# A sixth seven-product pair in each feed-forward duo of a decoder trunk, with a new order of its weight sums

## The chip, the cores and the metric

The kernel runs on one core of one Trainium2 chip. Its time is the device time in microseconds of one execution; runs of the kernel before gave 2178.22, 2179.26 and 2179.58 us, a median of 2179.26 us. The core has a matrix engine (PE, with its weight loads as PEld), a vector engine (DVE), an activation engine (ACT), GpSimd (POOL), a queue that issues transfers (SP), and DMA engines that move data from HBM.

## The reference, cut to what matters

```python
D_MODEL = 2048; SEQ = 256; D_FF = 5632      # one sequence of 256 tokens, float32

def swiglu(h, w_gate_up, w_down):
    gate, up = jnp.split(h @ w_gate_up, 2, axis=-1)
    return (jax.nn.silu(gate) * up) @ w_down

# layer 0: x += norm(GLA(norm(x)));        x += norm(swiglu(norm(x)))
# k, v = split(rmsnorm(x) @ w_kv)
# layer 1: x += norm(DiffAttn(norm(x)));   x += norm(swiglu(norm(x)))
```

Two layers, each a token mixer and a feed-forward block (SwiGLU). Each block has the products gate and up (2048 by 5632 each) and down (5632 by 2048). The change is in both feed-forward blocks and, in one detail, at the norm in front of the shared keys and values.

## The kernel before, in words

**Products.** Every float32 operand is split into a high and a low part (`hi`, `lo`, both float32r), and a product of a 128x128 piece of the activations with a 128x512 piece of the weights is three matmuls: high by high, high by low, low by high. Those three are called a product here. The activations are the stationary operand, the weights stream; a matmul streams 512 columns into an accumulator (`acc`, or `tp` where a transpose bank is borrowed).

**The weight stream.** Weights arrive in order as raw tiles of 128x1024 (two k-tiles of 512 columns, 512 KB each), issued from SP into five buffers (`NRAW`). Each becomes a unit: ACT copies the raw tile into `hi` (line 294), DVE subtracts it from the raw tile into `lo` (line 296), and PE uses both. Up to nine units are made ahead of PE (`NRING`). `take` hands a unit to PE and makes more, `free` gives its places back.

**A duo.** A chunk is 512 columns of gate or up. Eleven chunks each of gate and up make a block; chunk 0 is done by itself, and chunks 1 to 10 as duos: gate chunk c with up chunk 11+c, for both token halves (128 rows each), in eight steps s of two k-tiles. A plain step takes two units, one raw tile of each matrix, and does eight products. A fast step, or pair, computes the same with seven products on sums of weights and of activations (Strassen's scheme on a 2x2 block): its four units are a (the first raw tile as it is), b, c (1024 wide) and d (512 wide, in narrow places), where b, c and d are made of sums of the two raw tiles: DVE adds four 128x512 pieces (line 317, `sums`). The sums of activations are built once a block (`build_forms`, line 546). `FAST_FFN` lists the pairs of a duo, five of eight; chunk 1 has four (`FAST_SECOND`).

**After the steps.** When the last pair is done, DVE and ACT take five of the duo's seven accumulators apart (`early`, line 1129), and after step 7 the others (`late`), then Silu on ACT and gate times up on DVE (line 1133). PE transposes the result later (line 609), ACT and DVE split it (lines 611, 612).

**The order of a block.** Between two duos stands one part of the down products: eight units, twelve matmuls each (lines 370 to 372), with the running sums copied into accumulators by ACT before (line 423) and out after (line 1203). So from chunk 2 on the block is a row of nine spans, one duo with one part of down.

**What orders the instructions.** The program is written in the order PE consumes; helpers are put off by a count of ticks (`defer`), and a list scheduler with a cost model then sets the order on each engine. Each engine works its queue in order. `high_priority` lifts a helper, `issue_after(ins)` puts instructions of the same engine behind `ins` in the order, without a wait.

**The norm before the shared keys and values.** At the end of the first block the last units of down are skewed: all of the first token half, then all of the second. For each half, `after` calls the norm: DVE adds the block's output to x, PE transposes it, ACT and DVE scale and split it into `h_kv` (`scaled_T`, lines 644 to 650). PE then begins the value product with `h_kv`.

Of the kernel before, what the change touches and what calls it, by code (L numbers as in the profile page):

```python
# [18 lines left out]
P = 128  # L19
# [21 lines left out]
FAST_FFN = (0, 2, 3, 4, 6)  # L41
# [6 lines left out]
NRAW, NRING = 5, 9  # L48
V_BEGIN, V_EVERY, V_Q = 16, 3, 1
# [137 lines left out]
class Trunk:  # L187
    def __init__(self, ctx, tc, t):
# [16 lines left out]
        self.subs = {}  # L205
        self.raws = {}
# [83 lines left out]
    def split(self, src, gp=False):  # L290
        nc = self.nc
        w = src.shape[-1]
        hi, lo = self.places(w)
        nc.scalar.copy(hi, src)  # L294
        eng = nc.gpsimd if gp else nc.vector
        eng.tensor_tensor(out=lo, in0=src, in1=hi.bitcast(F32), op=ALU.subtract)  # L296
        return hi, lo
# [26 lines left out]

    def convert(self):
        n = self.n_conv
        kind = self.stream[n][2]
        self.n_done += kind in ("plain", "beside", "c", "b")
        if kind == "plain":
            self.subs[n] = self.split(self.raw(), n in self.pool_lo) if n else self.split_halves(self.raw())  # L330
        elif kind == "beside":
            self.subs[n] = self.split_beside(self.raw())
        elif kind == "a":
# [15 lines left out]
    def take(self, name, idx, kind="plain"):  # L349
# [4 lines left out]
        return self.subs.pop(n)  # L354

# [93 lines left out]
    def duo_act(self, aT, forms, fast, c1, c2, early, late):  # L449

        ps = [self.acc() for _ in range(6)] + [self.tp().rearrange("p j t -> p (j t)")]
        for s in range(8):
            k1, k2 = 2 * s, 2 * s + 1
            if s in fast:
# [18 lines left out]
                if last:  # L473
                    early(ps)
                continue
            for (w, n), pair in ((c1, ((1, 0), (3, 1))), (c2, ((4, 1), (2, 2)))):
                wp = self.take(w, (n, s))
                for bank, which in pair:
# [3 lines left out]
                    if s == 7:  # L482
                        late(bank, ps)
# [4 lines left out]
    def duo_apart(self, aT, forms, fast, chunks, early, late):  # L488
# [9 lines left out]
        for s in range(8):  # L498
            k1, k2 = 2 * s, 2 * s + 1
            if s not in fast:  # L500
                for (w, n), banks in zip(chunks, ((1, 3), (2, 7))):
                    wp = self.take(w, (n, s))
                    for b, bank in enumerate(banks):
# [4 lines left out]
                        if s == 7:  # L508
                            late(bank, ps)
                        self.tick()  # L510
                continue
            f, last = forms.pairs.index(s), s == fast[-1]
            plan = {
                "a": ((0, aT.tokens(k1, 0)), (1, aT.tokens(k2, 0))),
                "b": ((6, forms.fast(f, 2)), (2, forms.fast(f, 3))),
                "c": ((4, forms.fast(f, 0)), (3, aT.tokens(k2, 1))),
                "d": ((5, forms.fast(f, 1)),),
# [8 lines left out]
            if last:  # L526
                early(ps)
# [111 lines left out]

    def scaled_T(self, dst, b, c, xc, gi, plain=None):  # L640
# [8 lines left out]
        for j in range(4):  # L649
            nc.vector.scalar_tensor_tensor(  # L650
                out=lo[:, j, :], in0=tp[:, j, :], scalar=g[j], in1=hi[:, j, :].bitcast(F32),
                op0=ALU.mult, op1=ALU.subtract,
            )
        if plain is not None:
# [505 lines left out]
    def ffn(self, fp, hT, rs, gi, wgu, wd, post, after, name, reload, side=None):  # L1160
        nc = self.nc
        self.narrow, self.n_narrow = (fp, 0, 3), 0
# [10 lines left out]
        def gate_T(sg, c):  # L1173
# [3 lines left out]
            for b in range(2):  # L1177
                self.split_T(gTs[grp], 4 * grp.index(c), sg[:, b, :], b)
# [36 lines left out]
        for n, (kind, which, *chunks) in enumerate(plan):  # L1215
# [21 lines left out]
            def done(c, b, ps, grp=which):  # L1237
                (self.urgent(evac) if skew else evac)(grp, c, b, ps)
# [348 lines left out]
```

## Time and profile before

| | before |
|---|---|
| median of three runs | 2179.26 us |
| profiled execution | 2178.21 us |
| its span, first to last instruction | 2176.5 us |
| PE busy | 2161.2 us (99%) |
| DVE busy | 1889.5 us (87%) |
| ACT busy | 1341.4 us (62%) |
| transferred | 440.09 MB, 202 GB/s |

The profile is of one execution. Busy is the time in which an engine had at least one instruction under way; the durations of neighbours overlap, so the spacing of two starts is shorter than a duration. "Idle before" of an instruction is the engine's idle time just ahead of it, and the name behind the arrow is what ended it. Shares over the whole span mix stages of different limits, so a stage is read from its own window.

### The profile page before, as it was taken

To read this page: it belongs to the slowest core of one execution; us is meant where nothing else is said; L and a number is where in the kernel's file an instruction comes from. 1 tells how busy PE (TensorE), PEld (TensorE's weight loads), DVE (VectorE), ACT (ScalarE), POOL (GpSimd) and SP (SyncE) were. 2 spreads that over 40 slices of the span, in tenths; PEclk is the share of its full clock that TensorE was granted. 3 is DMA by queue.
4 is the path that set the end of the run, shared out by engine and by line. 5 is a ranking of instruction groups with operands and counts; after the bars stand their busy time and mean duration, and the time that the engine had idled before them with its cause. 6 is when DMAs were issued, how large, how long until landed. Compare 5 with 4: busy or idle time off the path is not lost.

```text
span 2176.5 us, 28464 instructions
## 1 busy us (share of the span) xinstructions
PE 2161.2 (99%) x10098; PEld 1797.6 (83%) x10098; DVE 1889.5 (87%) x2566; ACT 1341.4 (62%) x1888; POOL 36.3 (2%) x66
## 2 busy tenths in 40 slices
PE   9999999999999999999999999999999999999998
PEld 7887788888888888888788888888888888888886
DVE  7989988999899989988798567889998999899985
ACT  8656655666656666666676455556566666666664
POOL 1000000000000000000000000000000000000000
PEclk9999999999999999999999999999999999999999
DMA  8546566667655566565757655465656556566664
GB/s 309 168 150 191 176 228 212 215 212 246 204 179 193 198 213 212 195 222 191 239 189 245 189 172 164 149 233 195 230 197 221 189 178 197 204 209 220 204 212 136
DMA packets 123315, 440.09 MB, mean 202 GB/s; under 512 B 13899, under 2 KB 16628, under 8 KB 121380
## 3 DMA queue, kind: packets, MB, share of 16 engines
q1 hardware_dynamic: 121996, 436.44, 60.2%
q10 hardware_dynamic: 1176, 1.84, 0.2%
q8 instruction: 79, 1.29, 0.2%
q14 instruction: 64, 0.52, 0.1%
HBM read 429.82 MB, written 9.97 MB: 202 GB/s over the span
## 4 chain that ended last, share of the span: by engine, by line
PE 98%; DVE 1%; issue 0%; DMA 0%; ACT 0%; POOL 0%; SPq 0%; DVEq 0%; POOLq 0%; ACTq 0%
PE acc L445 13%; PE acc L447 13%; PE acc L446 13%; PE acc L372 11%; PE acc L370 11%; PE acc L371 11%; PE acc L588 8%; PE acc L589 4%; PE tp L445 3%; PE tp L446 3%; PE tp L447 3%; PE tp L609 1%; DVE lo L296 1%; PE acc L1310 0%; PE acc L1349 0%; PE tp L644 0%
## 5 line engine op out<-in xcount | busy, mean ns | idle before, releaser
L294 ACT CAST hi<-raw 128x1024 fp32r<-128x1024 f32 x905 | 929.7, 1051 | 568.2 <-DVE raw L317 227.2
L296 DVE TENSOR_TENSOR lo<-raw,hi 128x1024 fp32r<-128x1024 f32 x903 | 1079.6, 1219 | 182.2 <-ACT hi L294 179.4
L371 PE MATMUL acc<-lo,f_ffn_gT 128*128 128x512 f32 x704 | 273.7, 389 | 0.0
L370 PE MATMUL acc<-hi,f_ffn_gT 128*128 128x512 f32 x704 | 273.1, 390 | 0.0
L372 PE MATMUL acc<-hi,f_ffn_gT 128*128 128x512 f32 x704 | 268.5, 389 | 0.0
L445 PE MATMUL acc<-hi,h_ffn 128*128 128x512 f32 x666 | 259.3, 389 | 0.0
L447 PE MATMUL acc<-hi,h_ffn 128*128 128x512 f32 x666 | 259.3, 389 | 0.0
L446 PE MATMUL acc<-lo,h_ffn 128*128 128x512 f32 x666 | 259.1, 389 | 0.0
L372 PEld LDWEIGHTS acc<-hi,f_ffn_gT 128*128 128x128 f32 x704 | 132.2, 188 | 27.4
L370 PEld LDWEIGHTS acc<-hi,f_ffn_gT 128*128 128x128 f32 x704 | 132.0, 188 | 27.5 <-issue 0.6
L371 PEld LDWEIGHTS acc<-lo,f_ffn_gT 128*128 128x128 f32 x704 | 132.2, 188 | 27.1
L447 PEld LDWEIGHTS acc<-hi,h_ffn 128*128 128x128 f32 x666 | 125.0, 188 | 26.0
L446 PEld LDWEIGHTS acc<-lo,h_ffn 128*128 128x128 f32 x666 | 125.1, 188 | 25.9
L445 PEld LDWEIGHTS acc<-hi,h_ffn 128*128 128x128 f32 x666 | 125.0, 188 | 25.8
L588 PE MATMUL acc<-h_q,hi 128*128 128x512 f32 x256 | 92.6, 402 | 0.0
L588 PE MATMUL acc<-h_kv,hi 128*128 128x512 f32 x256 | 90.6, 399 | 0.0
L588 PE MATMUL acc<-h_mix,hi 128*128 128x512 f32 x256 | 90.6, 398 | 0.0
L317 DVE TENSOR_TENSOR raw<-sum,raw 128x512 f32<-128x512 f32 x122 | 84.3, 691 | 3.8
L317 DVE TENSOR_TENSOR raw<-raw 128x512 f32<-128x512 f32 x122 | 84.3, 691 | 3.6
L317 DVE TENSOR_TENSOR raw<-raw,raw 128x512 f32<-128x512 f32 x122 | 83.9, 687 | 2.3
L1203 ACT COPY f_ffn<-acc 128x512 f32<-128x512 f32 x80 | 46.9, 586 | 60.8 <-PE acc L372 60.6
L317 DVE TENSOR_TENSOR sum<-raw,raw 128x512 f32<-128x512 f32 x122 | 83.4, 684 | 0.0
(412 smaller groups left out, 3966.1 us busy)
## 6 DMA issues: line engine op xcount, KB each, us to landing
raw<-in_w_gu_dram SPq DMA_DIRECT2D x352, 512.0 KB, 4.5
raw<-in_w_d_dram SPq DMA_DIRECT2D x176, 512.0 KB, 4.9
raw<-in_gla_w_r_dram SPq DMA_DIRECT2D x32, 512.0 KB, 4.7
raw<-in_gla_w_v_dram SPq DMA_DIRECT2D x32, 512.0 KB, 4.0
raw<-in_gla_w_out_dram SPq DMA_DIRECT2D x32, 512.0 KB, 4.5
raw<-in_w_v_dram SPq DMA_DIRECT2D x32, 512.0 KB, 4.5
raw<-in_w_k_dram SPq DMA_DIRECT2D x32, 512.0 KB, 4.5
raw<-in_diff_w_q_dram SPq DMA_DIRECT2D x32, 512.0 KB, 4.2
```

The source lines that it names most:

```text
L294: nc.scalar.copy(hi, src)
L296: eng.tensor_tensor(out=lo, in0=src, in1=hi.bitcast(F32), op=ALU.subtract)
L317: nc.vector.tensor_tensor(out=out, in0=in0, in1=in1, op=ALU.add)
L370: nc.tensor.matmul(ps, ah, rh, start=(kt == 0 and not onto), stop=False, skip_group_check=onto)
L371: nc.tensor.matmul(ps, ah, rl, start=False, stop=False, skip_group_check=onto)
L372: nc.tensor.matmul(ps, al, rh, start=False, stop=(kt == 2 * ns - 1), skip_group_check=onto)
L445: nc.tensor.matmul(ps, ah, wh, start=first, stop=False)
L446: nc.tensor.matmul(ps, ah, wl, start=False, stop=False)
L447: nc.tensor.matmul(ps, al, wh, start=False, stop=last)
L588: nc.tensor.matmul(ps, lh, aT.both(kt), start=(kt == 0), stop=False)
L589: nc.tensor.matmul(ps[:, SEQ:], ll, aT.hi(kt), start=False, stop=(kt == KT - 1))
L1203: nc.scalar.copy(fc, ps)
```

## The change

Six things change.

1. `FAST_FFN` gets pair 5: steps 0, 2, 3, 4, 5 and 6 are fast, so that plain steps are 1 and 7 only. The sums of activations of one more pair are built.
2. For the feed-forward duos (weights whose name begins with `w_g`) the four weight sums are made by `convert_ffn`. The first sum goes into the narrow tile `sum` rather than over the raw tile, and is put behind unit a's low part on DVE; the second and fourth stay in place, the third is over the raw tile. Units c and d swap what they carry: the wide one now has bank 5 and form 1 beside bank 3, the narrow one bank 4 and form 0.
3. The narrow units have four places rather than three: two in a pool and two in the rest of a tile (before: three in the rest).
4. `early` and `late` of every duo, those outside the feed-forward blocks too, are put behind the cast and the low part of the latest unit made among those up to three ahead of PE (`behind`).
5. The low parts of weights are put behind the last low part of `h_kv` traced for the first token half (`split_off`, set in `scaled_T` only where x is kept too, which is this norm).
6. `GATE_BEHIND` and `DOWN_BEHIND` are 0 and do nothing.

The diff, cut:

```diff
-FAST_FFN = (0, 2, 3, 4, 6)
+FAST_FFN = (0, 2, 3, 4, 5, 6)
+EARLY_BEHIND, LATE_BEHIND, DOWN_BEHIND, GATE_BEHIND = 3, 3, 0, 0
+NEW_SUMS = ('w_g',)
...
-        hi, lo = self.places(w)
-        nc.scalar.copy(hi, src)
+        cast = nc.scalar.copy(hi, src)
         eng = nc.gpsimd if gp else nc.vector
-        eng.tensor_tensor(out=lo, in0=src, in1=hi.bitcast(F32), op=ALU.subtract)
+        with self.past(self.split_off):
+            rest = eng.tensor_tensor(out=lo, in0=src, in1=hi.bitcast(F32), op=ALU.subtract)
+        if not gp:
+            self.parts[self.n_conv] = cast.ins, rest.ins
...
+    def convert_ffn(self, kind):
+        if kind == "a":
+            self.pending = self.raw(), self.raw()
+            return self.split(self.pending[0])
+        if kind == "b":
+            r1, r2 = self.pending
+            t1 = self.narrow[0].tile([P, C], F32, tag="sum", name=self.uid("sum"))
+            self.pending = r1, r2, t1
+            with self.tc.issue_after(self.parts[self.n_conv - 1][1]):
+                self.add(t1, r1[:, :C], r2[:, :C])
+            self.add(r2[:, :C], r2[:, :C], r2[:, C:])
+            self.add(r1[:, :C], t1, r2[:, C:])
+            self.add(r1[:, C:], r1[:, :C], r1[:, C:])
+            return self.split(r2)
+        r1, r2, t1 = self.pending
+        return self.split(r1 if kind == "c" else t1)
...
+    def behind(self, ahead):
+        made = [n for n in self.parts if n < self.n_take + ahead]
+        if not made or not ahead:
+            yield
+            return
+        cast, rest = self.parts[max(made)]
+        with self.tc.issue_after(cast), self.tc.issue_after(rest):
+            yield
...
-                "c": ((4, forms.fast(f, 0)), (3, aT.tokens(k2, 1))),
-                "d": ((5, forms.fast(f, 1)),),
+                "c": ((5 if new else 4, forms.fast(f, 1 if new else 0)), (3, aT.tokens(k2, 1))),
+                "d": ((4 if new else 5, forms.fast(f, 0 if new else 1)),),
...
-                early(ps)
+                with self.behind(EARLY_BEHIND):
+                    early(ps)
...
+        if plain is not None and b == 0:
+            self.split_off = last.ins
...
-        self.narrow, self.n_narrow = (fp, 0, 3), 0
+        self.narrow, self.n_narrow = (fp, 2, 2), 0
```

Three places in the order. The first is DVE in one pair in the middle of a duo of the first block, from unit a's low part to the next unit's. In these rows `raw` are the two raw tiles, `lo` and `hi` are the parts of a unit, `f_ffn_rest` is a narrow place. Before:

```order
L296 TENSOR_TENSOR lo_6734<-raw_6584,hi_6733 128x1024
L317 TENSOR_TENSOR raw_6584<-raw_6584,raw_6634 128x512
L317 TENSOR_TENSOR raw_6634<-raw_6634 128x512
L317 TENSOR_TENSOR sum_6745<-raw_6584,raw_6634 128x512
L317 TENSOR_TENSOR raw_6584<-sum_6745,raw_6584 128x512
L296 TENSOR_TENSOR lo_6751<-raw_6634,hi_6750 128x1024
L296 TENSOR_TENSOR f_ffn_rest<-sum_6745,f_ffn_rest 128x512
L296 TENSOR_TENSOR lo_6761<-raw_6584,hi_6760 128x1024
L296 TENSOR_TENSOR lo_6794<-raw_6652,hi_6793 128x1024
```

The change, in the same pair:

```order
L301 TENSOR_TENSOR lo_6738<-raw_6584,hi_6737 128x1024
L333 TENSOR_TENSOR sum_6753<-raw_6584,raw_6633 128x512
L333 TENSOR_TENSOR raw_6633<-raw_6633 128x512
L333 TENSOR_TENSOR raw_6584<-sum_6753,raw_6633 128x512
L301 TENSOR_TENSOR lo_6793<-sum_6753,hi_6792 128x512
L333 TENSOR_TENSOR raw_6584<-raw_6584 128x512
L301 TENSOR_TENSOR lo_6759<-raw_6633,hi_6758 128x1024
L301 TENSOR_TENSOR lo_6779<-raw_6584,hi_6778 128x1024
L301 TENSOR_TENSOR lo_6805<-raw_6651,hi_6804 128x1024
```

The eight instructions of a pair are the same in kind; the narrow unit's low part now stands between the third and the fourth sum, and the first sum no longer writes the raw tile that unit a's low part reads.

The second place is DVE at the end of a duo, up to its third unit of down; `acc` and `tp` are the duo's accumulators, `sg` and `hs` the tiles of `early` and `late`. Before:

```order
L296 TENSOR_TENSOR lo_6441<-raw_6367,hi_6440 128x1024
L296 TENSOR_TENSOR lo_6453<-raw_6387,hi_6452 128x1024
L296 TENSOR_TENSOR lo_6465<-raw_6399,hi_6464 128x1024
L296 TENSOR_TENSOR lo_6477<-raw_6408,hi_6476 128x1024
L1129 TENSOR_TENSOR hs_6492<-acc_6234,sg_6491 128x512
L296 TENSOR_TENSOR lo_6486<-raw_6426,hi_6485 128x1024
L1129 TENSOR_TENSOR sg_6491<-tp_6203,hs_6492 128x512
L1129 TENSOR_TENSOR sg_6491<-acc_6182,sg_6491 128x512
L1129 TENSOR_TENSOR hs_6493<-acc_6215,sg_6491 128x512
L1129 TENSOR_TENSOR hs_6492<-acc_6215,hs_6492 128x512
```

The change, where the first row is the low part of the last pair's unit c:

```order
L301 TENSOR_TENSOR lo_6446<-raw_6297,hi_6445 128x1024
L301 TENSOR_TENSOR lo_6463<-raw_6359,hi_6462 128x1024
L301 TENSOR_TENSOR lo_6475<-raw_6393,hi_6474 128x1024
L301 TENSOR_TENSOR lo_6487<-raw_6405,hi_6486 128x1024
L1186 TENSOR_TENSOR hs_6559<-acc_6270,sg_6558 128x512
L301 TENSOR_TENSOR lo_6499<-raw_6437,hi_6498 128x1024
L1186 TENSOR_TENSOR sg_6558<-tp_6258,hs_6559 128x512
L1186 TENSOR_TENSOR sg_6558<-acc_6237,sg_6558 128x512
L301 TENSOR_TENSOR lo_6508<-raw_6449,hi_6507 128x1024
L1186 TENSOR_TENSOR hs_6560<-acc_6289,sg_6558 128x512
L1186 TENSOR_TENSOR hs_6559<-acc_6289,hs_6559 128x512
```

The low parts between the last pair and the first instruction of `early` are three in the change (before, eight, six of them of down), and the instructions of `early` and `late` stand spread among the units of down.

The third place is DVE at the norm before the shared keys and values, from the addition to x of the first token half on. Before:

```order
L687 SCALAR_TENSOR_TENSOR x_ffn_9168<-f_ffn_4427,st_9419,x_ffn_9168 128x512 x4
L296 TENSOR_TENSOR lo_9477<-raw_9309,hi_9476 128x1024
L1206 TENSOR_TENSOR f_ffn_4427<-acc_9358,gain_9353 128x512
L619 TENSOR_REDUCE st_9585<-st_3652 128x1
L296 TENSOR_TENSOR lo_9507<-raw_9327,hi_9506 128x1024
L296 TENSOR_TENSOR lo_9533<-raw_9351,hi_9532 128x1024
L296 TENSOR_TENSOR lo_9559<-raw_9440,hi_9558 128x1024
L620 TENSOR_SCALAR st_9585<-st_9585 128x1
L296 TENSOR_TENSOR lo_9571<-raw_9454,hi_9570 128x1024
L650 SCALAR_TENSOR_TENSOR h_kv_9424<-tp_9456,gcols,h_kv_9424 128x128 x4
```

The change:

```order
L744 SCALAR_TENSOR_TENSOR x_ffn_9307<-f_ffn_4438,st_9558,x_ffn_9307 128x512 x4
L1264 TENSOR_TENSOR f_ffn_4438<-acc_9497,gain_9492 128x512
L665 TENSOR_REDUCE st_9724<-st_3652 128x1
L666 TENSOR_SCALAR st_9724<-st_9724 128x1
L705 SCALAR_TENSOR_TENSOR h_kv_9563<-tp_9595,gcols,h_kv_9563 128x128 x4
L301 TENSOR_TENSOR lo_9616<-raw_9448,hi_9615 128x1024
L1264 TENSOR_TENSOR f_ffn_4438<-acc_9528,gain_9494 128x512
L670 TENSOR_SCALAR st_9724<-st_3652,st_9724 128x1
L705 SCALAR_TENSOR_TENSOR h_kv_9563<-tp_9621,gcols,h_kv_9563 128x128 x4
```

The five low parts of weights that stood ahead of the first `h_kv` row stand behind it.

More of the change, by code (lines that the diff above doesn't have):

```diff
@@ L1 @@
 import math
-from contextlib import ExitStack
+from contextlib import ExitStack, contextmanager
 import numpy as np
@@ L205, in __init__ @@
         self.subs = {}
+        self.split_off = None
+        self.parts = {}
         self.raws = {}
@@ L323, in sums, with add @@
         self.pending = r1, r2, t2
+    def add(self, out, in0, in1):
+        return self.nc.vector.tensor_tensor(out=out, in0=in0, in1=in1, op=ALU.add)
+    def convert_ffn(self, kind):
[14 more added lines that the diff above has]
+        return self.split(r1 if kind == "c" else t1)
     def convert(self):
@@ L482, in duo_act @@
                     if s == 7:
-                        late(bank, ps)
+                        with self.behind(LATE_BEHIND):
+                            late(bank, ps)
                     if bank in (2, 3):
@@ L508, in duo_apart @@
                         if s == 7:
-                            late(bank, ps)
+                            with self.behind(LATE_BEHIND):
+                                late(bank, ps)
                         self.tick()
@@ L512, in duo_apart @@
             f, last = forms.pairs.index(s), s == fast[-1]
+            new = chunks[0][0][:3] in NEW_SUMS
             plan = {
@@ L526, in duo_apart @@
             if last:
-                early(ps)
+                with self.behind(EARLY_BEHIND):
+                    early(ps)
     def rest_of(self, forms, i, name):
@@ L638, in gain, with past @@
         return g
+    @contextmanager
+    def past(self, ins):
+        if ins is None:
+            yield
+            return
+        with self.tc.issue_after(ins):
+            yield
     def scaled_T(self, dst, b, c, xc, gi, plain=None):
@@ L1177, in gate_T @@
             for b in range(2):
-                self.split_T(gTs[grp], 4 * grp.index(c), sg[:, b, :], b)
+                with self.behind(GATE_BEHIND):
+                    self.split_T(gTs[grp], 4 * grp.index(c), sg[:, b, :], b)
         def new_sg():
@@ L1237, in done @@
             def done(c, b, ps, grp=which):
-                (self.urgent(evac) if skew else evac)(grp, c, b, ps)
+                if skew:
+                    self.urgent(evac)(grp, c, b, ps)
+                else:
+                    with self.behind(DOWN_BEHIND):
+                        evac(grp, c, b, ps)
             base = None if which == first else part
```

5 lines of the change are left out of this document (4 added, 1 removed).

## The prediction

> **What bounds the kernel now.** I read the page first, then the waits and the busy time of one stretch in the middle of the first feed-forward block, then single instructions. The page gives the bound:
>
> ```profile
> PE 2161.2 (99%) x10098; PEld 1797.6 (83%) x10098; DVE 1889.5 (87%) x2566; ACT 1341.4 (62%) x1888; POOL 36.3 (2%) x66
> PE 98%; DVE 1%; issue 0%; DMA 0%; ACT 0%; POOL 0%; SPq 0%; DVEq 0%; POOLq 0%; ACTq 0%
> ```
>
> PE is busy 99% and carries 98% of the chain that ended last. So a matmul less is worth its spacing, as long as nothing else takes over. The candidate is DVE, at 87% on the mean. The mean hides the stage, so here is the stretch between two transposes two duos apart, and its waits:
>
> ```profile
> core 0: us, PE busy (x) PEld busy (x) DVE busy (x) ACT busy (x) POOL busy (x), PEclk, DMA share, GB/s
> 686.17:811.72 125.55, 125.55 (x564) 104.17 (x563) 114.45 (x132) 78.03 (x95) 0.00 (x0) 1.00 0.60 201
> DVE lo L296 <- ACT hi L294: 8.9, 13, 1.8
> DVE f_ffn_rest L296 <- ACT f_ffn_rest L294: 1.2, 1, 1.2
> ACT f_ffn L1203 <- PE acc L372: 7.0, 7, 4.3
> ACT hi L294 <- DMA raw<-in_w_d_dram: 6.0, 7, 1.7
> ```
>
> The columns of the second row are the length, then each engine's busy time. PE never stops. DVE is busy 114.45 of 125.55 us and waits 8.9 + 1.2 = 10.1 us; the missing 1.0 is the gaps between dependent neighbours. So a duo with its part of down takes 62.78 us of PE, and 125.55 - 10.1 = 115.45, or **57.73 us**, of DVE. DVE has 5.05 us to spare in each such span. The change spends most of that.
>
> **What PE saves.** A fast step is 7 products of three matmuls, a plain pair of units 8. Eighteen duos (chunks 2 to 10, two blocks) get one more fast step: 18 x 3 = 54 matmuls less. Their spacing:
>
> ```profile
> 705.71 0.39 PE L447 MATMUL acc<-hi,h_ffn 128*128 128x512 f32 x1
> ...
> 707.98 0.39 PE L445 MATMUL acc<-hi,f_ffn_fast 128*128 128x512 f32 x1
> ```
>
> Ten starts apart, 2.27 us: 0.227 each. 54 x 0.227 = **12.2 us**, 0.68 a span, so PE needs 62.10 us a span instead of 62.78. That is all the change can win in the blocks.
>
> **What DVE pays.** One fast step and the plain step after it, on DVE (start, duration):
>
> ```profile
> 757.92 0.69 DVE L317 TENSOR_TENSOR raw<-raw,raw 128x512 f32<-128x512 f32 x1
> 758.65 0.69 DVE L317 TENSOR_TENSOR raw<-raw 128x512 f32<-128x512 f32 x1
> 759.26 0.68 DVE L317 TENSOR_TENSOR sum<-raw,raw 128x512 f32<-128x512 f32 x1
> 759.98 0.69 DVE L317 TENSOR_TENSOR raw<-sum,raw 128x512 f32<-128x512 f32 x1
> 760.59 1.23 DVE L296 TENSOR_TENSOR lo<-raw,hi 128x1024 fp32r<-128x1024 f32 x1
> 761.73 0.69 DVE L296 TENSOR_TENSOR f_ffn_rest<-sum,f_ffn_rest 128x512 fp32r<-128x512 f32 x1
> 762.34 4.62 DVE L296 TENSOR_TENSOR lo<-raw,hi 128x1024 fp32r<-128x1024 f32 x4
> 766.99 0.69 DVE L317 TENSOR_TENSOR raw<-raw,raw 128x512 f32<-128x512 f32 x1
> ```
>
> From sum to sum it is 9.07 us, with two plain low parts in it. A low part in a run is (4.62 - 1.23) / 3 = 1.13 us apart, so the plain step is 2.27 and the fast step 6.80. One plain step becomes fast: +4.53 us a span. In the old order DVE would need 62.26, more than PE's 62.10.
>
> The new order takes some back. Sum 1 starts 1.25 us after the last low part (762.34 + 3 x 1.13 = 765.74 to 766.99) against 1.13 for an independent neighbour, since it overwrites what that one reads; into the narrow tile it need not: -0.12. Sums 1 to 2 and 3 to 4 are 0.72 apart, the others 0.61; the low part of d now stands between 3 and 4: -0.11. Against that, unit c's cast can start only after sum 4. From a sum's end to its cast 0.08 us, from a cast's end to its low part 0.03:
>
> ```profile
> 732.14 0.69 DVE L317 TENSOR_TENSOR raw<-raw 128x512 f32<-128x512 f32 x1
> 732.91 1.05 ACT L294 CAST hi<-raw 128x1024 fp32r<-128x1024 f32 x1 [4.30 <-DVE raw L317]
> 745.43 1.05 ACT L294 CAST hi<-raw 128x1024 fp32r<-128x1024 f32 x1
> 746.51 1.23 DVE L296 TENSOR_TENSOR lo<-raw,hi 128x1024 fp32r<-128x1024 f32 x1 [0.26 <-ACT hi L294]
> ```
>
> So c's low part can start 0.69 + 0.08 + 1.05 + 0.03 = 1.85 us after sum 4 starts, and DVE gets there after 0.61 + 1.13 = 1.74: +0.10. Net -0.13 in each of six pairs, -0.78. DVE work is then 57.73 + 4.53 - 0.78 = **61.5 us against PE's 62.1**. It fits by 0.6 us, and against the old span by 1.28. Everything hangs on how many of the 5.05 idle microseconds are left over. If the savings of the new order fail, it fits by nothing.
>
> [...]
>
> **What is left of DVE's idle time.** It comes from two places in a span: where units of down wait for their transfers, and where ACT stands in a copy out of an accumulator that PE has not finished, with casts queued behind it.
>
> ```profile
> 715.99 1.22 DVE L296 TENSOR_TENSOR lo<-raw,hi 128x1024 fp32r<-128x1024 f32 x1 [1.18 <-ACT hi L294]
> 717.74 1.22 DVE L296 TENSOR_TENSOR lo<-raw,hi 128x1024 fp32r<-128x1024 f32 x1 [0.52 <-ACT hi L294]
> 719.29 1.22 DVE L296 TENSOR_TENSOR lo<-raw,hi 128x1024 fp32r<-128x1024 f32 x1 [0.33 <-ACT hi L294]
> 720.76 1.23 DVE L296 TENSOR_TENSOR lo<-raw,hi 128x1024 fp32r<-128x1024 f32 x1 [0.25 <-ACT hi L294]
> 744.43 0.59 ACT L1203 COPY f_ffn<-acc 128x512 f32<-128x512 f32 x1 [4.34 <-PE acc L372]
> 745.57 0.69 DVE L296 TENSOR_TENSOR f_ffn_rest<-sum,f_ffn_rest 128x512 fp32r<-128x512 f32 x1 [1.15 <-ACT f_ffn_rest L294]
> 748.27 2.55 DVE L296 TENSOR_TENSOR lo<-raw,hi 128x1024 fp32r<-128x1024 f32 x2 [0.53 <-ACT hi L294]
> raw<-in_w_d_dram SPq DMA_DIRECT2D x16, 512.0 KB, 4.9
> ```
>
> Transfers: 1.18 + 0.52 + 0.33 + 0.25 = 2.28 us, while eight low parts stand in a row. In the new order three do, and the instructions of the duo's end lie between the rest. With five raw buffers, the second unit of down is sent for when unit b of the last pair is done; DVE comes to it 1.14 + 3 x 1.13 + 0.61 = 5.1 us later, and it is ready after 4.9 + 1.05 = 5.95. So 0.8 us there and nothing behind it; below, 0, if the transfer is quick, above, the whole 2.28. I take 0.4, between nothing and my reckoning. Copies: 1.15 + 0.26 + 0.53 = 1.94 us. DVE waited here because it was ahead of PE; some 5 us later in its work (4.53 + 0.68), it finds the copy's 4.34 us wait over. Bounds 0 and 1.94; I take 0.45, nearer to 0 for that reason. Together 0.85 us a span, 0.25 more than fits: PE loses 18 x 0.25 = **4.5 us** of its 12.2.
>
> **Smaller terms.** The sums of a sixth pair of activations are made while DVE has no room:
>
> ```profile
> 410.00:435.00 25.00, 25.00 (x112) 20.70 (x111) 24.27 (x44) 11.65 (x15) 0.00 (x0) 1.00 0.60 198
> L546 DVE TENSOR_TENSOR f_ffn_temp<-f_ffn_temp 128x128 f32<-128x128 f32 x20 | 5.0, 278 | 0.1
> ```
>
> The second row is from the window 385 to 436 us: 20 instructions, five pairs of four, 1.0 us a pair, and two 512-wide ones of 0.6. These 2.2 us push DVE back once a block; PE's supply made ahead covers most. 0 to 2.2, taken 0.4, twice: +0.8. The swap of banks, the places of narrow units and the order of `early` and `late` elsewhere add no instruction; PE stood still nowhere near them, so 0; if that cover went, a stall would be of the size of one low part, 1.2 us.
>
> The norm before the shared keys and values has PE's only long stop:
>
> ```profile
> 1082.75 3.48 DVE L296 TENSOR_TENSOR lo<-raw,hi 128x1024 fp32r<-128x1024 f32 x3
> 1087.35 2.15 DVE L650 SCALAR_TENSOR_TENSOR h_kv<-tp,gcols,h_kv 128x128 fp32r<-128x128 f32 x8
> 1083.90 2.17 ACT L648 ACTIVATE h_kv<-tp,gcols 128x128 fp32r<-128x128 f32 x8
> 1087.75 0.49 PE L372 MATMUL acc<-hi,h_kv 128*128 128x512 f32 x1 [2.27 <-DVE h_kv L650]
> 1094.91 0.50 PE L372 MATMUL acc<-hi,h_kv 128*128 128x512 f32 x1 [0.49 <-DVE h_kv L650]
> ```
>
> ACT has the first four at about 1085.0, DVE only comes at 1087.35, behind weights. With those behind it, the 2.27 us go. But the 1094.91 stop does not depend on them: its h_kv follows the second half's addition to x, so PE arrives up to 2.3 us sooner and waits longer. DVE gets to it about 1 us sooner (two weights ahead of it rather than six, but it starts later). I take -1.2; bounds -2.76 (both gone) and +1 (a weight wanted by then is late).
>
> **The sum.** Against the profiled execution's 2178.21 us (span 2176.5 and 1.7 around it): -12.2 + 4.5 + 0.8 - 1.2 = -8.1, so 2170.1. The median of the runs is 1.05 us above that execution, so **2171 us**, 0.4% faster.
>
> **The rivals.** First, slower: **transfers keep DVE idle**. Place: the units of down in each span. If the low parts catch up as fast as before, five buffers cannot feed them, and 2.28 us stay. It decides from 1.28 us idle a span on. Then DVE needs 61.5 + 2.28 = 63.78, 1.0 more than the old span: 18 us, less 0.4 of the small terms: 2197; with 1.9 us idle, 2190. For it: the 6.0 us that ACT waited on these transfers. Against it: the catching up is spread by the instructions between. Chance 0.26.
>
> Second, **a draw**: idle time of 1.1 to 1.4 us, or the new order does not save its 0.78. Then DVE's 62.26 with 0.5 us is the old span, and the norm alone is left: 2175 to 2183, middle 2179. Chance 0.19.
>
> Third, **no overlap on DVE** once it runs without a pause. Full durations are 0.08 us more than the spacing (0.69 against 0.61). The 66 instructions of a span would cost 5.3 us more and the added step 4 x 0.69 + 0.69 + 1.22 = 4.67: 57.73 + 5.3 + 4.7 = 67.7 us, 4.9 over the old span, 88 us in all, 2267. The quoted rows overlap in a stretch without a pause; 0.01.
>
> **How the numbers follow.** My case, DVE just keeping up, has 0.54: from 2165 (no idle beyond 0.6: -12.2 - 1.2 + 1.05, nothing for the sums) to 2175. A run of this kernel tells a change of about 0.2%, 4.4 us, from none. So faster 0.54, within 0.20, slower 0.26. The range for 8 in 10 runs from 2164 to 2190: the bottom takes in the whole gain at PE and at the norm, the top the slower rival up to 1.9 us idle; its rest and less than 2164 are left out.
>
> **What would show it.** In the changed profile: PE instructions 54 fewer, and a span between like transposes of 62.1 to 62.5 us. DVE busy in two spans about 122 us. PE gaps, if any, short, ended by DVE's low parts, at steps 5 to 7 of a duo, where the run of pairs is longest. DVE idle on casts below 2 us in two spans. The fourth sum right behind d's low part, 0.61 us. At the norm a stop below 0.5 us where 2.27 was, and a longer one for the second half. I would be wrong if PE stands still over 1.3 us a span, if DVE idles over 2.5 us in two spans while PE waits for it, or if pairs take DVE 6.8 us still.

## The result, and the profile after

| kernel | runs | median, us | range, us |
|---|---|---|---|
| before | 4 | 2179.37 | 2178.22 to 2179.58 |
| changed | 4 | 2168.33 | 2167.76 to 2168.64 |

The ratio is 0.9951, with a 95% interval of 0.9939 to 0.9963: the change makes the kernel 11.0 us, 0.5%, faster. The prediction was 2171, from 2164 to 2190.

The page of the changed kernel has the same bound as before. Here are its busy line and the shares of its chain of waits:

```profile
PE 2151.2 (99%) x10044; PEld 1787.7 (83%) x10044; DVE 1953.3 (90%) x2686; ACT 1374.2 (63%) x1926; POOL 37.1 (2%) x66
PE 93%; DVE 4%; issue 1%; ACT 1%; DMA 1%; SPq 0%; POOL 0%; DVEq 0%; POOLq 0%; ACTq 0%
```

There are 54 PE instructions fewer (10098 to 10044). DVE is up from 1889.5 to 1953.3 us, and it now holds 4% of the chain where it held 1%: the reserve is thinner.

The stretch between like transposes, two duos with their parts of down, shows what the change does where nothing disturbs it (busy times in the order PE, PEld, DVE, ACT, POOL), and then what its engines wait for (us, times, longest):

```profile
684.31:808.49 124.18, 124.18 (x557) 103.00 (x556) 121.09 (x144) 81.32 (x98) 0.00 (x0) 1.00 0.60 204
```

```profile
DVE f_ffn_rest L301 <- ACT f_ffn_rest L298: 1.5, 1, 1.5
DVE f_ffn_gT L658 <- ACT f_ffn_gT L657: 0.7, 2, 0.5
...
ACT hi L298 <- DMA raw<-in_w_d_dram: 3.7, 6, 1.2
```

It is 124.18 us long where it was 125.55: 62.09 a span, and PE does not stop once. DVE is busy 121.09 us of it and waits for casts 1.5 us and for the transposes' casts 0.7, where it waited 10.1. ACT waits 3.7 us for transfers of weights of down, where it waited 6.0.

In DVE's own order, a pair now looks like this (start, duration):

```profile
690.77 0.69 DVE L333 TENSOR_TENSOR sum<-raw,raw 128x512 f32<-128x512 f32 x1
691.49 0.69 DVE L333 TENSOR_TENSOR raw<-raw 128x512 f32<-128x512 f32 x1
692.10 0.69 DVE L333 TENSOR_TENSOR raw<-sum,raw 128x512 f32<-128x512 f32 x1
692.70 0.68 DVE L301 TENSOR_TENSOR lo<-sum,hi 128x512 fp32r<-128x512 f32 x1
693.30 0.68 DVE L333 TENSOR_TENSOR raw<-raw 128x512 f32<-128x512 f32 x1
693.91 3.64 DVE L301 TENSOR_TENSOR lo<-raw,hi 128x1024 fp32r<-128x1024 f32 x3
697.47 0.69 DVE L333 TENSOR_TENSOR sum<-raw,raw 128x512 f32<-128x512 f32 x1
```

From first sum to first sum it is 6.70 us (the next pair is 6.68), against 6.80 in the old order. The fourth sum starts 0.60 us behind d's low part.

What that leaves is seen in the last pair of the duo. The first row is DVE with the low parts behind the fourth sum, the others are PE with the second product of two of these units:

```profile
713.98 5.91 DVE L301 TENSOR_TENSOR lo<-raw,hi 128x1024 fp32r<-128x1024 f32 x5
...
716.02 0.39 PE L487 MATMUL tp<-lo,f_ffn_rest 128*128 128x512 f32 x1
...
717.15 0.39 PE L487 MATMUL acc<-lo,f_ffn_rest 128*128 128x512 f32 x1
```

The first low part of that row ends 1.22 us after its start, at 715.20, and PE takes it at 716.02; the second ends at 716.49 and is taken at 717.15. So DVE is **0.67 us** ahead of PE there. In the next duo the same place is 1.62 us ahead. In the trace of before the smallest distance in these pairs is 7.0 us, at unit c of the fourth pair: its low part is the first of this row of DVE and ends at 701.20, and PE takes it at 708.20:

```profile
699.98 4.62 DVE L296 TENSOR_TENSOR lo<-raw,hi 128x1024 fp32r<-128x1024 f32 x4
...
708.20 0.39 PE L446 MATMUL acc<-lo,f_ffn_fast 128*128 128x512 f32 x1
```

PE stands still where it did not before, or not as long, at the end of the tenth duo and at the norm behind the first block (the number in brackets is the idle time before the row):

```profile
1046.30 0.88 PE L655 MATMUL tp<-ident,sg 128*128 128x128 f32 x6 [1.01 <-DVE sg L1190]
1081.78 0.50 PE L413 MATMUL acc<-hi,h_kv 128*128 128x512 f32 x1 [0.43 <-DVE h_kv L705]
1089.54 0.50 PE L413 MATMUL acc<-hi,h_kv 128*128 128x512 f32 x1 [1.11 <-DVE h_kv L705]
1091.27 0.66 PE L699 MATMUL tp<-ident,x_ffn 128*128 128x128 f32 x4 [0.30 <-ACT x_T L712]
```

The first is new: the transposes of the last gate chunk wait for DVE's gated product. The second block has a smaller one at the same place, 0.31 us. The others are the norm before the shared keys and values: 0.43 where 2.27 us were, 1.11 where 0.49 were, and 0.30 at its transposes.

By stages, from the starts of PE's first and last matmuls of each kind, the time went here:

| stage | before, us | changed, us |
|---|---|---|
| up to the first feed-forward matmul | 384.88 | 385.10 |
| first feed-forward, to the last matmul of down | 699.64 | 694.81 |
| norm and values, to the first matmul of the keys | 90.87 | 90.60 |
| shared keys, then queries | 201.56 | 201.41 |
| from there to the second feed-forward | 92.47 | 92.46 |
| second feed-forward | 697.99 | 692.96 |

Nine spans of 0.68 us saved are 6.1 us a block; 4.8 and 5.0 arrived. The seven spans that end with the transposes of the ninth duo give all of it: in both blocks they take 434.65 us for 439.41, 7 x 0.68 less. Nearly all of what is missing is lost behind them. A shift between two stages also counts: four of the norm's 32 transposes of x (28 for 24) now start behind the last matmul of down, so they are timed in the norm's stage and not in the block's.

### The profile page after: what moved, and what is told of

Same layout as the page of the kernel before. It is cut to its first block, busy times and chain, and to the rows that moved or that the text cites. A ratio compares the mean times of both kernels' runs of the same rounds, so it can differ in the third digit from the quotient of the medians.

```text
span 2166.4 us, 28415 instructions
## 1 busy us (share of the span) xinstructions
PE 2151.2 (99%) x10044; PEld 1787.7 (83%) x10044; DVE 1953.3 (90%) x2686; ACT 1374.2 (63%) x1926; POOL 37.1 (2%) x66
## 3 DMA queue, kind: packets, MB, share of 16 engines
q10 hardware_dynamic: 1176, 1.84, 0.2%
## 4 chain that ended last, share of the span: by engine, by line
PE 93%; DVE 4%; issue 1%; ACT 1%; DMA 1%; SPq 0%; POOL 0%; DVEq 0%; POOLq 0%; ACTq 0%
PE acc L488 12%; PE acc L487 12%; PE acc L486 12%; PE acc L413 11%; PE acc L412 11%; PE acc L411 11%; PE acc L634 8%; PE acc L635 4%; PE tp L487 2%; PE tp L486 2%; PE tp L488 2%; DVE lo L301 2%; PE tp L655 1%; DVE raw L333 1%; DMA raw<-in_w_d_dram 1%
## 5 line engine op out<-in xcount | busy, mean ns | idle before, releaser
L301 DVE TENSOR_TENSOR lo<-raw,hi 128x1024 fp32r<-128x1024 f32 x921 | 1096.2, 1220 | 115.1 <-ACT hi L298 108.8
L298 ACT CAST hi<-raw 128x1024 fp32r<-128x1024 f32 x923 | 943.9, 1051 | 356.5 <-DVE raw L333 91.5
L487 PE MATMUL acc<-lo,h_ffn 128*128 128x512 f32 x612 | 238.7, 390 | 0.0
L488 PE MATMUL acc<-hi,h_ffn 128*128 128x512 f32 x612 | 238.4, 389 | 0.0
L486 PE MATMUL acc<-hi,h_ffn 128*128 128x512 f32 x612 | 227.8, 390 | 0.0
L333 DVE TENSOR_TENSOR raw<-raw 128x512 f32<-128x512 f32 x232 | 159.5, 687 | 3.4
L486 PEld LDWEIGHTS acc<-hi,h_ffn 128*128 128x128 f32 x612 | 114.9, 188 | 24.2 <-ACT hi L298 0.4
L488 PEld LDWEIGHTS acc<-hi,h_ffn 128*128 128x128 f32 x612 | 114.9, 188 | 23.5
L487 PEld LDWEIGHTS acc<-lo,h_ffn 128*128 128x128 f32 x612 | 114.9, 188 | 23.5
L298 ACT CAST hi<-sum 128x512 fp32r<-128x512 f32 x72 | 44.8, 622 | 101.1 <-DVE sum L333 101.1
L298 ACT CAST f_ffn_rest<-sum 128x512 fp32r<-128x512 f32 x56 | 34.9, 623 | 80.9 <-DVE sum L333 80.9
```

The source lines that it names most:

```text
L298: cast = nc.scalar.copy(hi, src)
L301: rest = eng.tensor_tensor(out=lo, in0=src, in1=hi.bitcast(F32), op=ALU.subtract)
L333: return self.nc.vector.tensor_tensor(out=out, in0=in0, in1=in1, op=ALU.add)
L486: nc.tensor.matmul(ps, ah, wh, start=first, stop=False)
L487: nc.tensor.matmul(ps, ah, wl, start=False, stop=False)
L488: nc.tensor.matmul(ps, al, wh, start=False, stop=last)
```

## The experiments

All were timed beside the kernel before on the same chip. "To before" is the difference of the medians of one such comparison, "to changed" that number less the -11.0 us of the changed kernel.

| run | what it is | median, us | ratio to before, 95% interval | to before, us | to changed, us |
|---|---|---|---|---|---|
| e1 | five pairs, all orders new | 2176.76 | 0.9990 (0.9981 to 0.9999) | -2.2 | +8.8 |
| e2 | old sums | 2183.20 | 1.0020 (1.0011 to 1.0029) | +4.2 | +15.3 |
| e3 | early and late free | 2190.19 | 1.0056 (1.0043 to 1.0069) | +11.2 | +22.3 |
| e4 | late reload | 2163.42 | 0.9930 (0.9917 to 0.9942) | -15.5 | -4.5 |
| e5 | no tie | 2172.82 | 0.9970 (0.9960 to 0.9981) | -5.8 | +5.2 |
| e6 | sixth pair alone | 2215.26 | 1.0167 (1.0153 to 1.0181) | +36.6 | +47.7 |
| e7 | one sum more in a duo | 2174.09 | 0.9980 (0.9972 to 0.9989) | -4.5 | +6.5 |
| e8 | three sums more in a duo | 2189.87 | 1.0051 (1.0037 to 1.0064) | +11.2 | +22.3 |
| e9 | before, late reload | 2179.37 | 0.9999 (0.9990 to 1.0008) | +0.1 | |
| e10 | before, with the tie | 2177.53 | 0.9993 (0.9984 to 1.0002) | -1.7 | |
| e11 | late reload, second chunk with five pairs | 2169.09 | 0.9958 (0.9944 to 0.9971) | -10.2 | +0.9 |

**e1: five pairs, everything else of the change.**

```diff
-FAST_FFN = (0, 2, 3, 4, 5, 6)
+FAST_FFN = (0, 2, 3, 4, 6)
```

> Five pairs a duo as before, with everything else of the change: the new order of sums, the swapped banks, early and late behind the low parts, the tie at the norm. Theory (the pair is what pays; the rest, beside the norm, is worth nothing while PE is the bound): PE instructions back to 10098, only the 0.9 us that the norm's two stops lost (2.76 before, 1.84 now) remain: 2178.5 us, 2177.5 to 2179.5. Rival (the orders themselves free PE): 2175 or less.

Measured: 2176.76 us, a little under the lower bound of the first theory, and over the rival's. With the orders in place, the sixth pair is worth 8.8 us of the 11.0. Of the other 2.2 the trace shows 1.75 at the norm: its stage, with the values, takes 89.12 us against 90.87. Both feed-forward blocks are as long as before or a little longer (699.82 and 698.36). There the new orders win nothing.

**e10: the tie alone, on the kernel before.**

```diff
 FAST_FFN = (0, 2, 3, 4, 6)
-EARLY_BEHIND, LATE_BEHIND, DOWN_BEHIND, GATE_BEHIND = 3, 3, 0, 0
-NEW_SUMS = ('w_g',)
+EARLY_BEHIND, LATE_BEHIND, DOWN_BEHIND, GATE_BEHIND = 0, 0, 0, 0
+NEW_SUMS = ()
```

> The kernel before with the tie at the norm and nothing else: five pairs, old order of sums, early free. The run with five pairs and all the orders was 2.2 us faster than before. Theory (with five pairs the tie is all of that, since DVE is 7 us ahead and no order matters): 2176.8 us, 2176 to 2177.5. Rival (the orders gained or lost something even there): more than 1 us away from 2176.8.

Measured: 2177.53 us, 1.7 us less than before on that chip, against e1's 2.2; the interval of the ratio just reaches 1. The two agree within half a microsecond. The stage of the norm and the values takes 90.02 us in its trace, 0.85 less. Its blocks take 699.64 and 697.95 us, those of before 699.64 and 697.99. With five pairs, no order matters in the blocks. The four places of the narrow units are still in this kernel, so they too cost and gain nothing there.

**e2: six pairs, sums in the old order.**

```diff
-NEW_SUMS = ('w_g',)
+NEW_SUMS = ()
```

> Six pairs, but the sums in the old order. A pair should take DVE 0.11 us more (6.80 against 6.69 from sum to sum). Theory (what DVE is ahead of PE at the end of the pairs, 0.67 us at the least, is a reserve that is filled again in every span from idle time): six times 0.11 is 0.66, the reserve goes to about 0 and PE loses little: 2168.5 to 2171 us. Rival (the prediction's sum, where DVE fits by 0.6 us only thanks to the new order): the 0.66 us of a span become PE's, 18 x 0.66 = 12, 2180 us.

With the old sums, units c and d carry again what they carried before. Measured: 2183.20 us, over even the rival's 2180. The sixth pair in the old order is slower than five. A pair takes 6.79 us from sum to sum in its trace, 0.10 more. PE now arrives before the low parts of the last pair, the place that had 0.67 us to spare:

```profile
715.17 0.44 PE L486 MATMUL acc<-f_ffn_rest 128*128 128x512 f32 x1
715.86 0.50 PE L487 MATMUL tp<-lo,f_ffn_rest 128*128 128x512 f32 x1 [0.24 <-DVE lo L301]
```

These starts are 0.69 us apart, where 0.23 is the rule. And DVE, though late, waits again, as this row of its waits in the two spans from 684 to 810 us shows:

```profile
DVE f_ffn_gT L658 <- ACT f_ffn_gT L657: 2.0, 1, 2.0
```

Two spans take 125.57 us, the next two 127.60. So PE loses 0.85 us a span on the mean (389.6 us against 384.3 over the 6.2 spans between the first block's like transposes), for 0.6 us of added DVE time. The price is more than the length. Over the whole run PE's longest waits here are not those for low parts (1.9 us in all) but these, for ACT's part of the transposed gated product, in front of units of down:

```profile
PE acc L411 <- ACT f_ffn_gT L657: 6.7, 8, 1.8
```

The longest of the first block, 1.84 us, stands in the second of the two stretches. So a late DVE makes other work late as well; through which instructions was not taken apart.

**e7 and e8: the same time on DVE, without another order.** The first sum of a pair is made twice; what is computed stays the same.

```diff
             with self.tc.issue_after(self.parts[self.n_conv - 1][1]):
                 self.add(t1, r1[:, :C], r2[:, :C])
+            c1, _, step = self.stream[self.n_conv][1]
+            if step in (3,) and c1[1] > 1:          # e8: (2, 3, 4)
+                self.add(t1, r1[:, :C], r2[:, :C])
```

> The changed kernel, with the first weight sum of one pair in each duo from the third chunk on made twice, 18 sums more; the result is the same. Theory (DVE is full: what idle time it has left cannot be used, as in the old order of sums): 0.61 to 0.72 us in each of 18 spans reach PE in full, 2179 to 2182 us. Rival (the old order costs by what it holds up, not by its length, and there are 0.6 us to spare as the prediction had it): 2168.5 to 2170.5.

> The same in three pairs of each duo, 54 sums more. Theory (DVE is full): three times the price of one, 33 to 39 us, 2201 to 2207. Rival (a reserve of 0.6 us a span, then full price): 1.2 to 1.5 us a span, 22 to 27 us, 2190 to 2195.

Measured: 2174.09 and 2189.87 us, +6.5 and +22.3. e7 lies between its theories; e8 is at the lower edge of the rival with a reserve. The doubled sum in the order of DVE in e7:

```profile
690.45 1.41 DVE L333 TENSOR_TENSOR sum<-raw,raw 128x512 f32<-128x512 f32 x2
691.90 0.69 DVE L333 TENSOR_TENSOR raw<-raw 128x512 f32<-128x512 f32 x1
```

Two spans of e7, and then of e8:

```profile
683.99:808.75 124.76, 124.47 (x557) 102.93 (x556) 122.47 (x146) 81.50 (x98) 0.00 (x0) 1.00 0.59 202
```

```profile
687.82:815.00 127.18, 125.35 (x558) 102.70 (x557) 125.18 (x151) 81.51 (x98) 0.00 (x0) 1.00 0.60 200
```

What DVE waits for in these two spans of e8, all of it, and PE's stops in the first of them:

```profile
DVE f_ffn_gT L661 <- ACT f_ffn_gT L660: 0.8, 1, 0.8
```

```profile
719.09 0.50 PE L489 MATMUL tp<-hi,f_ffn_rest 128*128 128x512 f32 x1 [0.70 <-ACT hi L298]
720.84 0.50 PE L489 MATMUL acc<-hi,f_ffn_rest 128*128 128x512 f32 x1 [0.58 <-ACT hi L298]
```

The next sum starts 1.45 us after the doubled one, 0.72 after the single one: the copy costs DVE 0.73. Over two spans e7 adds 1.46 and loses 0.58; e8 adds 4.38 and loses 3.00. So the changed kernel has 0.88 to 1.38 us of reserve in two spans, 0.4 to 0.7 a span. The whole of it is not to be had by a first sum, which fits the two duos being not equally far ahead (0.67 and 1.62 us): in e7 one half of the two spans still takes 73.88 us as in the changed kernel, the other 50.89 for 50.31. In e8, DVE is full. It needs 127.18 - 4.38 = 122.8 us for two spans of the changed kernel's work, its last waits among them: **61.4 us a span, 0.7 less than PE's 62.09**.

**e3: early and late not behind the low parts.**

```diff
-EARLY_BEHIND, LATE_BEHIND, DOWN_BEHIND, GATE_BEHIND = 3, 3, 0, 0
+EARLY_BEHIND, LATE_BEHIND, DOWN_BEHIND, GATE_BEHIND = 0, 0, 0, 0
```

> Everything of the change but early and late: their instructions are no longer held behind the next three low parts. Theory of the prediction (this order costs and gains nothing): within 1.5 us of the changed kernel, 2167 to 2170. Rival (with a reserve of 0.67 us the order is what makes six pairs possible): ACT's copy out of the first accumulator now stands ahead of four casts and waits for PE; 1 to 2 us of it reach PE in each of 18 to 20 duos, 2188 to 2208 us.

Measured: 2190.19 us, +22.3: the rival. The rows at the end of a duo are ACT's copy of the first accumulator and the casts behind it, then DVE, then PE:

```profile
718.62 0.59 ACT L1197 COPY sg<-acc 128x512 f32<-128x512 f32 x1 [2.14 <-PE acc L488]
719.24 0.59 ACT L464 COPY acc<-f_ffn 128x512 f32<-128x512 f32 x1
719.76 4.84 ACT L298 CAST hi<-raw 128x1024 fp32r<-128x1024 f32 x5
...
720.84 3.50 DVE L301 TENSOR_TENSOR lo<-raw,hi 128x1024 fp32r<-128x1024 f32 x3 [2.65 <-ACT hi L298]
...
721.81 0.50 PE L486 MATMUL acc<-hi,h_ffn 128*128 128x512 f32 x1 [0.21 <-ACT hi L298]
...
741.32 1.09 PE L655 MATMUL tp<-ident,sg 128*128 128x128 f32 x8 [0.56 <-DVE sg L1190]
...
743.62 0.50 PE L411 MATMUL acc<-hi,f_ffn_gT 128*128 128x512 f32 x1 [1.20 <-ACT f_ffn_gT L657]
```

ACT waits 2.14 us for PE with the next units' casts behind it, DVE waits 2.65 for these casts, and what DVE then makes late (the gated product, then the transposes) stops PE, far from the cause. Here a wait on an engine that is busy 63% of the time decides. Only `early` does it: with `late` alone set free, the program that is built is the same, instruction for instruction.

**e6: the sixth pair alone**, with all three edits undone (e2's, e3's and e5's). The four places of the narrow units stay.

> The sixth pair alone: old order of sums, early and late free, no tie. The old sums alone cost 14.8 us and the free early and late alone 21.8 against the changed kernel. Theory (two shortages of different engines, DVE's time and ACT's place in the queue, add up): 2168.3 + 14.8 + 21.8 + 0.9 = 2206 us, 2200 to 2210. Rival (one shortage counted twice, since DVE that is late finds ACT's copy already over): 2185 to 2195. The prediction's own view of a pair without the new order was a draw, 2175 to 2183.

Measured: 2215.26 us, +47.7. Both theories are wrong, the first by less: the single prices add up to 15.3 + 22.3 + 5.2 = 42.8. The longest waits of PE are the casts that e3 had:

```profile
PE tp L486 <- ACT hi L298: 15.7, 9, 1.8
PE acc L411 <- ACT f_ffn_gT L657: 5.9, 8, 1.9
```

In e3 they were 0.5 us at the most in front of these matmuls. The reading that fits, not tested further: in the sums' old order PE comes to these casts with nothing in hand, and the stop of e3 reaches it directly, up to 1.8 us at a time.

**e5: no tie.**

```diff
-        if plain is not None and b == 0:
-            self.split_off = last.ins
```

> The changed kernel without the tie: low parts of weights no longer wait for the first half's part of the norm before the shared keys and values. Theory (the prediction's size for the tie): the stops at the norm grow from 1.84 us back to about 2.8, 2169.2 us, 2168.5 to 2170.5. Rival (the DVE queue is so full at the norm that the tie moves as much as it saves): no difference, 2168.3.

Measured: 2172.82 us, +5.2, over both theories. The stops at the norm:

```profile
1080.68 0.50 PE L411 MATMUL acc<-hi,h_kv 128*128 128x512 f32 x1 [1.17 <-ACT h_kv L703]
...
1084.15 0.80 PE L413 MATMUL acc<-hi,h_kv 128*128 128x512 f32 x1 [2.73 <-DVE h_kv L705]
```

That is 3.9 us, more than the 2.76 that the kernel before had without a tie. Five low parts of weights stand ahead of the first `h_kv` row of DVE here, as many as before, so their number is not the reason; the stop of 1.17 us is one for ACT's part, which before had none. Why it comes late was not taken apart. The tie saves 2.1 us of these stops. From the last matmul of down to the first of the keys it is 95.19 us for 90.60, while the first block ends 1.2 sooner: the stop of 1.01 us at its tenth duo is missing in this trace, and all 32 transposes of x stand behind the last matmul of down, for 28. The net 3.4 is what the trace shows, and the rest of the 5.2 lies within the runs' spread (2171.02 to 2174.47).

**e4: the reload of x behind seven weights of down.** The one new stop in the blocks is at the end of the tenth duo. SP's queue there, and what it waits for, in the changed kernel:

```profile
1000.21 13.72 SPq L263 DMA_DIRECT2D raw<-in_w_gu_dram  x5
1018.97 0.80 SPq L1463 DMA_DIRECT2D x_ffn<-x_mix  x2
1019.87 0.38 SPq L263 DMA_DIRECT2D raw<-in_w_gu_dram  x1
1020.35 29.66 SPq L263 DMA_DIRECT2D raw<-in_w_d_dram  x16
```

```profile
SPq L1463 <- PE acc L488: 5.0, 1, 5.0
```

The reload overwrites the pairs' sums of activations, so SP stands 5.0 us until PE has read the last of them, with the last gate weight and the first weights of down queued behind it; then the reload's 2 MB go first. What DVE waits for a little later:

```profile
1028.88 1.06 ACT L298 CAST hi<-raw 128x1024 fp32r<-128x1024 f32 x1 [0.25 <-DMA raw<-in_w_d_dram]
...
1031.61 1.05 ACT L298 CAST hi<-raw 128x1024 fp32r<-128x1024 f32 x1 [1.20 <-DMA raw<-in_w_d_dram]
...
1032.69 1.23 DVE L301 TENSOR_TENSOR lo<-raw,hi 128x1024 fp32r<-128x1024 f32 x1 [0.90 <-ACT hi L298]
```

The experiment moves the reload on SP only:

```diff
-        self.nc.sync.dma_start(raw, self.t[name][idx])
+        self.sent = self.sent[-7:] + [self.nc.sync.dma_start(raw, self.t[name][idx]).ins]
...
-                    reload()
+                    with self.past(self.sent[0]): reload()
```

> The changed kernel, with the reload of x before the last two chunks of down placed on SP behind seven weights of down, where it stood ahead of the last weight of gate and waited 5.0 us for PE. Theory (the stop at the last gate transposes, 1.0 us and more in the first block and 0.7 in the second, comes from transfers that the reload holds up): no stop over 0.3 us there, and 1.5 to 2 us less, 2166.3 to 2167.2. Rival (the stop is the price of DVE's full queue at the end of ten duos): the stop stays, 2168 to 2169.

Measured: 2163.42 us, 4.5 less than the changed kernel, the fastest of all: 0.9930 of the time before. In its trace SP has the reload without a wait and PE the transposes without a stop:

```profile
1020.02 12.16 SPq L263 DMA_DIRECT2D raw<-in_w_d_dram  x7
1032.23 0.91 SPq L1463 DMA_DIRECT2D x_ffn<-x_mix  x2
...
1044.35 1.03 PE L655 MATMUL tp<-ident,sg 128*128 128x128 f32 x8
```

The stop is gone as the theory had it. The distance to the transposes before falls from 51.52 to 49.85 us in the first block and from 50.83 to 49.85 in the second, but these are not stops alone, since the transposes also stand two matmuls earlier in PE's order, and a wait of 0.2 to 0.3 us for ACT's part comes behind them instead. The gain is more than the 1.5 to 2 us expected, and by the stages most of it lies elsewhere: 0.4 us in each block, 2.2 between the last matmul of down and the first of the keys (the norm's three stops are one of 0.78, and four transposes of x are timed in the block again), 1.5 in the keys, 0.3 in the queries, 0.4 before the first block, which the edit does not touch. That of the keys is no stop at all and is told at the end.

Nor does the reload make the stop by itself. In e5's trace SP waits the same 5.0 us in the same place, and PE comes to the transposes of the first block with 0.01 us idle. The cast for which DVE waits 0.90 us in the profile of the changed kernel starts 5.9 us after its tile was sent for; the same cast in e5 starts 4.9 us after. So a transfer that was slower by 1 us in that execution has its part in the stop, on top of the reload.

**e9: the same late reload on the kernel before.**

The edit is that of e4.

> The kernel before, with the reload of x behind seven weights of down as in the run with the late reload (before, it stands behind two). Theory (that order pays because six pairs leave nothing in hand at the end of ten duos; the kernel before is 7 us ahead there): nothing in the feed-forward blocks, 2177.5 to 2179.5 us. Rival (it pays anywhere: the norm and the values behind it get their weights sooner): 4 to 5 us less, 2173.5 to 2175.5.

Measured: 2179.37 us, no difference (+0.1). But the reload's wait that the edit takes away is a shorter one here, in the kernel before:

```profile
SPq L1401 <- PE acc L447: 1.3, 1, 1.3
```

So 2 MB in front of the weights of down and 1.3 us of waiting cost nothing while DVE is some 7 us ahead. What 5.0 us of waiting would cost there is not shown, and neither is which of the two, the longer wait or the thinner lead, gives the reload its price with six pairs.

**e11: a pair more in the second chunk**, on top of the late reload, to see whether the reserve there can be spent.

```diff
-FAST_SECOND = (0, 2, 4, 6)
+FAST_SECOND = (0, 2, 3, 4, 6)
```

> The changed kernel with the late reload and five pairs in place of four in the second chunk (both blocks), 6 matmuls less. Theory (DVE's lead is 5.2 us at the least there and 2.5 in the next duo; a pair more takes 4.43 - 0.68 = 3.75 of it and a span gives back 0.7): 0.6 us of stop in the third chunk against 0.68 gained, in each block, so 2163 to 2164 us, no gain. Rival (the lead is rebuilt from idle time faster than that): 2161.5 to 2162.5. Rival (a late DVE holds up more than itself, as with the old order of sums): 2165 or more.

Measured: 2169.09 us, 5.4 more than e4 by the differences to before: the last rival. But it is so only in the first block, 699.66 us for 694.42. In the second, 692.71 for 692.52, the first theory's balance holds. In the first, the work for the bias table stands at that place:

```profile
483.88 1.09 PE L655 MATMUL tp<-ident,sg 128*128 128x128 f32 x8 [2.62 <-DVE sg L1190]
485.62 0.81 PE L816 MATMUL acc<-hs,tab 33*8 33x384 f32 x2 [0.65 <-DMA hs<-in_onehot_dram]
```

A stop of 2.62 us is seen where the theory had 0.6; that the bias table's work is what makes the difference was not tried.

## Why the prediction was right, and where it was not

**What PE saves** was right: 54 instructions fewer and 62.09 us a span, for 62.10.

**What DVE pays** was right within some 0.5 us: 61.5 forecast; e8 gives 61.4 with the 0.4 us of waits a span that were left there, 61.0 without. The new order saves 0.10 to 0.12 us a pair, not 0.13 (6.68 to 6.70 us against 6.80, forecast 6.67): the wait for c's cast is 0.17 where 0.10 was taken (three low parts in 3.56 us, 693.91 to 697.47, against 3 x 1.13 = 3.39).

**What is left of DVE's idle time** is the term that was mis-sized: 0.85 us a span, 0.25 more than fits, 4.5 us in all. In the changed kernel DVE idles 1.1 us a span on casts (1.5 and 0.7 in two), more than forecast and over the 2 us in two spans that were to be its sign, and yet none of it reaches PE. With more work on DVE it shrinks: in the full state of e8 only 0.4 us a span are left (0.8 in two spans, in its row for the transposes' casts). So idle time of this kind was not lost time to be added to the work. The reasoning was right that the transfers' waits go when the low parts do not stand in a row any more and that DVE comes later to the copies' waits; it took too much to be left over once DVE is full. The 0.85 was an estimate between bounds of 0 and 4.22 us a span, and 0.6, the point from which idle time was to cost, lay well inside.

**The sums of the sixth pair of activations** were taken at 0.8 us. PE has no stop over 0.2 us between 390 and 610 us in the first block: 0.

**The norm** went as told: the 2.27 us stop fell to 0.43, the other grew from 0.49 to 1.11. By stops it is -0.9, timed alone on the kernel before it is -1.7 (e10); the forecast was -1.2. What the prediction did not see is that the stops would be 3.9 us in the changed kernel without the tie (e5), so that the tie is worth more there than on the kernel before. It is not the sixth pair by itself that makes them longer: with the pair and none of the orders they are 2.5 us (e6).

**The step that failed** as a reason is the one that put the order of `early` and `late` at 0, "PE stood still nowhere near them", and 1.2 us if the cover went. The cover did go: it was the 7.0 us that DVE was ahead, of which 0.67 are left in the changed kernel. Without the new place of `early` the changed kernel takes 22.3 us more (e3). The 0 was right for the time of the changed kernel, as the edit adds nothing; as a reason it was wrong, because the edit prevents a loss twice as large as the gain. The instruction to look at was the ACT copy that waits for PE, and the casts queued behind it.

**The rivals.** The draw said that the new order of sums decides. It does, beside the place of `early`: without it the time is 2183.20 us (e2), 0.2 over that rival's upper end. But the reckoning behind it, length against length, is not enough: 0.6 us a span cost 0.85 when they come with the old order, and 0.73 cost 0.29 when they come as one more sum (e7). What the old order holds up besides was not taken apart. The rival that transfers keep DVE idle was wrong for the spans. It was right at one place that it did not name, the end of the tenth duo, where DVE waits 0.90 us for the cast of a tile that is late and PE then stops for 1.01 and 0.31 us in the two blocks. The rival of no overlap on DVE is out: with DVE full (e8), independent neighbours start 0.60 us apart and last 0.68 to 0.69. The Trainium skill, VectorE: DVE Perf Modes, section The DRAIN you can't avoid, has the next operation start only when the pipe of the one before is empty, and adds that a next operation that is not held starts earlier. These neighbours do start earlier, by 0.08 us.

**The sum.** By the stages it is -12.2 at PE, +2.4 that do not arrive in the two blocks (6.1 less 4.8, 6.1 less 5.0), and -0.3 in the norm's stage: -10.1, as between the two profiled spans; the medians differ by 11.0. Of the 2.4, the recorded stops at the tenth duos are 1.01 and 0.31. The late reload brings back 0.4 us a block, and what makes the rest was not taken apart. The forecast was -8.1 between the profiled spans. It lost 4.5 in the ordinary spans and 0.8 at the activations, where nothing was lost; against that, it lost nothing behind the ninth duos and took 0.9 too much for the norm's stage. So that 2171 lies within 2.7 us of the measured median is in part luck, since losses in the wrong place stood in for others. That the changed kernel would be faster, with PE the bound in every ordinary span and DVE just keeping up, was right by its reasons.

## What to carry to other kernels

When work is moved onto an engine that has time to spare, ask how far ahead of its consumer it is at the worst point of each stage, since that distance hides every badly placed wait; once it is spent, orders that had cost nothing have a price: 15 and 22 us here. So price the protecting edits by undoing them one at a time under the new load, not under the old one. And look where a queue waits for a buffer with other transfers behind it: moving that was worth 4.5 us after the change, 1.5 of them by a spacing of matmuls that is not explained, and nothing before it, where the wait was 1.3 us for 5.0.

## What the runs showed of the hardware

Two spacings of the same matmuls. In the stage of the shared keys PE makes matmuls 512 and 256 wide in turn, in the changed kernel with starts 0.24, 0.12, 0.24, 0.11, 0.23 and 0.12 us apart, over and over; with the late reload it is 0.23 and 0.12 throughout. Busy time and instructions of 40 us of it, of the changed kernel and then of the one with the late reload:

```profile
1190.00:1230.00 40.00, 40.00 (x229) 34.67 (x228) 22.04 (x26) 16.58 (x21) 0.00 (x0) 1.00 0.61 189
```

```profile
1190.00:1230.00 40.00, 40.00 (x233) 35.28 (x232) 22.30 (x26) 17.32 (x22) 0.00 (x0) 1.00 0.61 187
```

PE is busy all the time at a granted clock of 1.00 in both, and does 229 matmuls in one and 233 in the other. Over the stage of 512 matmuls that is 90.77 against 89.24 us, with the same order on PE but for one small product one place earlier. All kernels here take 90.75 to 90.77 us for it, but e4 and e11, the two with six pairs and the late reload, take 89.24. What chooses between the two is open. A difference of 1.5 us between kernels that differ elsewhere can come from this alone, and a third of e4's gain does.

An operation of DVE on 128x512 that writes what its neighbour has just written (e7's doubled sum) starts 0.72 us after it, one that overwrites what its neighbour reads also 0.72 (the second sum of a pair), an independent one 0.60. Each lasts 0.69.
